# A two-layer hybrid encoder on one core: gate projections moved ahead of a norm, output projections moved into the sliding attention, and a decay matrix built by selection

## The chip, the cores and the metric

The kernel runs on one core of a Trainium2 chip. The metric is the device time of one execution in microseconds (us); the median of three runs counts. A core has TensorE (PE, matrix products), VectorE (DVE), ScalarE (ACT) and GpSimd (POOL), each with its own queue of instructions that it works off in order, and SyncE (SP), whose queue issues most of the DMA transfers.

## The reference

Two groups of tokens (1024 of a prompt, 512 of a sample, width 1024, fp32) go through two layers and a last RMSNorm. Cut to what matters here:

```python
# layer 0
u = rmsnorm(x) @ w_in                          # glu, a_gate, q, k, v, b_gate
a = a_val * sigmoid(a_glu)
a = layernorm(depthwise_conv(a, 31 taps))      # over channels
a = silu(a) * silu(a_gate)
o = windowed_gqa(rope(q), rope(k), v, sink) * silu(b_gate)   # +-128 tokens
x = x + concat([a, o]) @ w_out
# layer 1
u = rmsnorm(x) @ w_in                          # q, k, v, c_gate, z, xbc, dt_f, dt_b
c = diff_attention(q, k, v, lam) * silu(c_gate)
d = mamba2_bidir(z, xbc, softplus(dt_f + b), softplus(dt_b + b))
x = x + concat([c, d]) @ w_out
# in mamba2_bidir, per block of 128 tokens and direction (the backward one on flipped tokens)
decay[l, s] = exp(a_cum[l] - a_cum[s]) if l >= s else 0
y_diag = (C B^T * decay) @ (x * dt)            # and y = y_f + y_b + x * d_skip
```

## The kernel before

The 1536 tokens form three chunks of 512: g = 0 and 1 are the prompt, g = 2 the sample. Every fp32 product is split into high and low halves: the projection of one chunk onto 128 columns is 8 x 3 = 24 matmuls of 128 x 512 (`proj`, lines L294 to L296: high by high, high weight by low input, low weight by high input). `load_w` brings the weights in two halves (DMA), ACT rounds the high half (L282) and POOL subtracts the low half (L283). `split_into` does the same for inputs: ACT copies (L215), DVE or POOL subtracts (L216).

The program is written in phases, each with a set of SBUF and PSUM pools (`PHASES`, numbers of buffers per name). A tile scheduler decides the order on each engine from what is written; a buffer that is not yet free delays whoever wants it next.

Phase A1 computes the gated input, the convolution (taps on DVE and ACT, its last sum in L486), q, k and v, then the convolution's norm (`conv_ln`: first a matmul with a mean matrix, L494) and the first two groups of gates, `ag(0)` and `ag(1)`; a group is 128 channels for three chunks, 72 matmuls.

Phase A2 is the sliding attention: `swa_units` gives 24 units (12 blocks of 128 queries, two key heads), each of which computes scores (L568, L569), their row maximum (DVE, L572), exponentials (ACT, L574), scales them (POOL, L582), and for the unit before it transposes (L597), splits (L216) and multiplies with the values (L600, L601). The sample's 8 units come first, then the prompt's 16. `spread` puts other work between the units: groups of gates (`ag`, `bg`), and for `so[g]`, the output projection of chunk g, first the loading and multiplying of its 8 input tiles (`so[g][1]`, `cat_units`: two loads from DRAM, L626 and L629, a product on DVE, L630, and the split) and then its 8 projections (`so[g][2]`, 192 matmuls; L643 loads the residual, L644 adds, L654 squares, L655 sums the squares). The numbers in the table passed to `spread` are the units between which the work is written. The attention's output goes through DRAM (L605) before `cat_units` reads it.

Phase B1a does the rest of the output projections, each followed by `out_norm` (the next layer's norm: L668 loads, L669 scales, L216 splits), then `dtproj` (the 16 step sizes, on 40 columns, 24 matmuls per chunk) and the `xbc` projections. B1z holds two groups of token-major projections. B1b is the state-space scan, with projections of layer 1's attention between its blocks. Per block (12 of them) and direction, two matmuls (L872) write the exponents of 4 heads each into PSUM (`sg`), a second matmul with the identity adds a large negative number in the half that is to vanish (L873), ACT takes the exponential of all 8 heads (L876, 1024 columns), DVE adds the two directions (L878) and multiplies with C B^T (L883); 8 matmuls with x follow (L888). B2 is the differential attention and O1 the last output projection.

## Time and profile before

| | |
|---|---|
| median of three runs | 1650.86 us (1645.56, 1650.86, 1658.24) |
| the profiled execution | 1646.57 us |
| its span, first to last instruction | 1644.8 us |
| PE, DVE, ACT, POOL busy | 94%, 66%, 45%, 41% |
| mean granted clock of PE | 0.987 |

The profile is of one execution. Busy shares are means over stages of different kinds; the table of busy time by stretch parts them. An engine's idle time is given with the instruction that ended it. Matmuls overlap, so the time of one is longer than the step from one start to the next. The granted clock is a share of the full 2.4 GHz.

### The profile page before, as it was taken

Reading aid. Unit: us, or ns where it says so; the run is one execution under the profiler, and the core shown is the slowest. Engines: PE = TensorE matmul, PEld = TensorE weight load, DVE = VectorE, ACT = ScalarE, POOL = GpSimd, SP = SyncE. Lnnn points to the kernel's source line nnn. Section 1 sums busy time; section 2 is a strip of 40 time slices with the busy share of each in tenths; the row PEclk is TensorE's granted clock in tenths of the full one; section 3 lists DMA queues with packets and bytes.
Section 4 is the critical chain, followed back from the end, with each engine's and each line's share of the span. In section 5 each row is a group of like instructions: output and inputs, shape, how many; then the busy total and the mean of one; then the engine's idle time right before and its main releaser. Section 6 shows DMA issues by size and latency. Waiting matters only on the chain.

```text
span 1644.8 us, 22557 instructions
## 1 busy us (share of the span) xinstructions
PE 1541.7 (94%) x7772; PEld 1280.1 (78%) x7772; DVE 1092.4 (66%) x1568; ACT 747.4 (45%) x1461; POOL 670.8 (41%) x555
## 2 busy tenths in 40 slices
PE   4999899699989899999999999999989999999897
PEld 3888787478857777778788888878878888888787
DVE  6699999866688857565542005786537678678663
ACT  6312111266777754345442112222227777668532
POOL 4333543226766647432211006654435535341530
PEclk9999999899999999999999999999999999999999
DMA  9221123244556558613333217754454445342561
GB/s 371 70 68 42 45 84 92 94 159 143 162 172 192 167 165 264 203 58 91 112 126 116 77 45 218 212 173 152 133 172 139 142 152 167 116 133 73 182 232 67
DMA packets 159108, 229.43 MB, mean 139 GB/s; under 512 B 18279, under 2 KB 70567, under 8 KB 158994
## 3 DMA queue, kind: packets, MB, share of 16 engines
q1 hardware_dynamic: 157074, 227.40, 43.8%
q8 instruction: 61, 1.00, 0.3%
q0 software_dynamic: 1920, 0.59, 0.2%
q14 instruction: 53, 0.43, 0.1%
HBM read 153.15 MB, written 64.55 MB: 132 GB/s over the span
## 4 chain that ended last, share of the span: by engine, by line
PE 34%; DMA 5%; DVE 4%; issue 3%; ACT 2%; POOL 2%; SPq 1%; POOLq 0%; DVEq 0%; ACTq 0%
PE pj L294 4%; PE pj L295 4%; PE pj L296 4%; PE ms L994 3%; PE pjx L759 2%; PE pjx L760 2%; PE pjx L761 2%; PE s L978 2%; PE s L979 2%; PE pjx L296 2%; PE pjx L295 2%; PE pjx L294 2%; PE tr L406 1%; PE trx L406 1%; DMA ct<-g2d 1%
## 5 line engine op out<-in xcount | busy, mean ns | idle before, releaser
L283 POOL TENSOR_TENSOR wl<-wr,wh 128x512 fp32r<-128x512 f32 (+1 forms) x147 | 210.1, 1433 | 277.7 <-ACT wh L282 265.6
L295 PE MATMUL pjx<-x,wh 128*128 128x512 f32 (+1 forms) x576 | 227.6, 395 | 5.6 <-DVE x L216 5.6
L294 PE MATMUL pjx<-x,wh 128*128 128x512 f32 (+1 forms) x576 | 228.3, 397 | 3.0 <-DVE e L395 1.0
L296 PE MATMUL pjx<-x,wl 128*128 128x512 f32 (+1 forms) x576 | 227.7, 396 | 3.3 <-POOL wl L283 3.3
L294 PE MATMUL pj<-x,wh 128*128 128x512 f32 x536 | 215.8, 403 | 12.5 <-ACT e L387 4.4
L295 PE MATMUL pj<-x,wh 128*128 128x512 f32 x536 | 211.8, 395 | 4.5 <-DVE x L216 4.5
L296 PE MATMUL pj<-x,wl 128*128 128x512 f32 x536 | 213.1, 398 | 0.0
L282 ACT ACTIVATE wh<-wr 128x512 fp32r<-128x512 f32 (+1 forms) x147 | 91.5, 623 | 130.5 <-PE pjx L295 49.4
L295 PEld LDWEIGHTS pjx<-x,wh 128*128 128x128 f32 (+1 forms) x576 | 107.4, 186 | 30.8 <-DVE x L216 6.8
L294 PEld LDWEIGHTS pj<-x,wh 128*128 128x128 f32 x536 | 101.8, 190 | 37.1 <-ACT e L387 6.4
L294 PEld LDWEIGHTS pjx<-x,wh 128*128 128x128 f32 (+1 forms) x576 | 107.3, 186 | 29.3 <-ACT x L215 1.8
L296 PEld LDWEIGHTS pjx<-x,wl 128*128 128x128 f32 (+1 forms) x576 | 107.1, 186 | 28.0 <-POOL wl L283 4.1
L295 PEld LDWEIGHTS pj<-x,wh 128*128 128x128 f32 x536 | 101.7, 190 | 25.9 <-DVE x L216 6.0
L296 PEld LDWEIGHTS pj<-x,wl 128*128 128x128 f32 x536 | 101.7, 190 | 21.5 <-issue 0.5
L980 DVE TENSOR_REDUCE nmx<-s 128x1 f32<-128x1024 f32 (+1 forms) x96 | 97.9, 1040 | 23.5 <-PE s L979 23.0
L982 ACT ACTIVATE pr<-s,nmx 128x1024 f32<-128x1024 f32 (+1 forms) x96 | 93.4, 975 | 32.7 <-DVE nmx L980 29.1
L191 POOL TENSOR_TENSOR r<-v,mhalf 128x4 f32<-128x4 f32 (+2 forms) x37 | 33.4, 901 | 128.8 <-DVE v L187 76.5
L994 PEld LDWEIGHTS ms<-v,pT 128*128 128x128 f32 x640 | 78.5, 191 | 6.8 <-ACT m L996 2.0
L994 PE MATMUL ms<-v,pT 128*128 128x128 f32 x640 | 81.3, 276 | 2.2 <-ACT m L996 1.2
L532 POOL TENSOR_TENSOR raw<-raw,q 128x1024 fp32r<-128x1024 f32 x24 | 59.1, 2462 | 49.3 <-ACT q L530 38.7
L836 POOL TENSOR_TENSOR xd<-x,ed 128x512 f32<-128x512 f32 x20 | 23.2, 1161 | 125.5 <-DMA x<-xbd 120.6
L283 POOL TENSOR_TENSOR wlx<-wrx,whx 128x512 fp32r<-128x512 f32 x20 | 51.4, 2578 | 55.4 <-ACT whx L282 55.4
(415 smaller groups left out, 3786.9 us busy)
## 6 DMA issues: line engine op xcount, KB each, us to landing
wr<-in_wo SPq DMA_DIRECT2D x84, 256.0 KB, 4.2
wr<-in_w SPq DMA_DIRECT2D x71, 256.0 KB, 3.6
x<-xbd SPq DMA_DIRECT2D x22, 384.0 KB, 4.4
ct<-x1d SPq DMA_DIRECT2D x29, 256.0 KB, 4.3
raw<-q0d SPq DMA_DIRECT2D x48, 128.0 KB, 3.1
ct<-cat0d SPq DMA_DIRECT2D x24, 256.0 KB, 4.7
x1d<-e SPq DMA_DIRECT2D x24, 256.0 KB, 3.9
raw<-q1d SPq DMA_DIRECT2D x48, 128.0 KB, 2.8
```

Source lines behind the costliest of these rows:

```text
L191: G.tensor_tensor(out=r[:, 0:n], in0=v[:, 0:n], in1=mhalf[:, 0:n], op=ALU.pow)
L282: S.activation(out=wh, in_=raw, func=AF.Copy)
L283: G.tensor_tensor(out=wl, in0=raw, in1=wh.bitcast(F32), op=ALU.subtract)
L294: T_.matmul(acc, wh[:, kk, :], xh[:, k, :], start=(k == ks[0]), stop=False)
L295: T_.matmul(acc, wh[:, kk, :], xl[:, k, :], start=False, stop=False)
L296: T_.matmul(acc, wl[:, kk, :], xh[:, k, :], start=False, stop=(k == ks[-1]))
L406: T_.transpose(pt[:, t, :], src[:, t * P:(t + 1) * P], ident)
L532: G.tensor_tensor(out=lo, in0=raw, in1=q.bitcast(F32), op=ALU.subtract)
L759: T_.matmul(acc, xh[:, k, ts], hi[k], start=(k == 0), stop=False)
L980: V.tensor_reduce(out=nmx[:, t:t + 1], in_=o, axis=AX.XY, op=ALU.max, negate=True)
L982: S.activation(out=pr, in_=o, func=AF.Exp, bias=nmx[:, t:t + 1], accum_out=den[:, t:t + 1])
L994: T_.matmul(oacc, pT[:, i, :], vtok[:, kt, :], start=(kt == 0), stop=(kt == NB - 1))
```

## The change

1. The gate group `ag(2)` is written with `ag(0)` and `ag(1)` ahead of the convolution's norm, and the first mean matmul is tied to come after the last matmul of these three groups; `ag(3)` follows.
2. In A2 the pools change, the work between units is tied to the first score matmul of the unit written last, and its table changes: chunk 2's output projections come at 13 to 20, chunk 0's input tiles at 18 to 21 and its 8 projections at 20 to 26 (before: in B1a). Chunk 0's norm factor is computed at the end of A2.
3. `dtproj` packs the high and low weights into 128 columns, so that a chunk takes 16 matmuls; ACT copies the lower part of the result and DVE adds it.
4. In B1b the identity matmuls go. Both directions' exponents of 4 heads are written to two PSUM tiles, DVE copies the backward ones over the forward ones where a constant mask says so (`copy_predicated`, 128 x 512), and ACT takes one exponential of the result; the sum of the two directions goes. The diagonal of the backward direction is added to `d_skip`: two DVE reductions over C B^T times the identity and two small POOL operations per block. `rk` has four buffers for two.
5. Two constant tiles that served the identity matmuls are no longer made.

The core of the diff (left out: constants, the packing of the dt weights on the host, the copy of `rk` four times for two):

```diff
-    "A2": (dict(raw=3, v2=1, k4=3, v4=1, ct=3, ss=1, m2=1, sq=1, pT=5, pr=10, q6=2), dict(pjx=1, s1=3, trx=1)),
+    "A2": (dict(raw=3, q6=2, k2=2, v2=1, m2=1, pr=9, pT=5, k4=2, v4=1, ct=3, ss=2, sq=1), dict(pjx=1, s1=3, trx=1)),
...
-    "B1b": (dict(e2x=1, wrx=1, whx=1, wlx=1, rk=2, lk=4, cs=2, p4=4, x3=2, bc=2, xd=2, y=2, t=1, nx=4, pb=1, yc=2, zt=1), dict(sg=1, msx=2, trx=1)),
+    "B1b": (dict(e2x=1, wrx=1, whx=1, wlx=1, rk=4, lk=4, cs=2, p4=2, jk=1, x3=2, bc=2, xd=2, y=2, t=1, nx=4, pb=1, yc=2, zt=1), dict(sg=2, msx=2, trx=1)),
...
-                T_.matmul(acc, wl[:, kk, :], xh[:, k, :], start=False, stop=(k == ks[-1]))
+                ph["proj"] = T_.matmul(acc, wl[:, kk, :], xh[:, k, :], start=False, stop=(k == ks[-1]))
...
-    def conv_ln():
+    def conv_ln(pin):
         sm = cvs["s"]
         for g in GO:
             mu = pm("ms")
-            T_.matmul(mu, mean_w, sm[:, g, :], start=True, stop=True)
+            with tc.issue_after(pin.ins):
+                T_.matmul(mu, mean_w, sm[:, g, :], start=True, stop=True)
...
-            kt = sb("k4", (P, T), F32R)
+            kt = sb("k2" if T == CH and "k2" in ph["sb"] else "k4", (P, T), F32R)
...
-                T_.matmul(o, qh[:, g, j, :], kk[g][:, k0 * P:k1 * P], start=True, stop=False)
+                first = T_.matmul(o, qh[:, g, j, :], kk[g][:, k0 * P:k1 * P], start=True, stop=False)
                 T_.matmul(o, ql[:, g, j, :], kk[g][:, k0 * P:k1 * P], start=False, stop=True)
+                if j == 0:
+                    ph["pin"] = first
...
+    def norm_r(st_):
+        st_["r"] = rstd_of(tok_sum([st_["ss"]]), 4, 1.0 / DM)
+
     def out_norm(st_, spill, g, gcol, last):
-        bc = tok_bcast(rstd_of(tok_sum([st_["ss"]]), 4, 1.0 / DM), 4, False)
+        if "r" not in st_:
+            norm_r(st_)
+        bc = tok_bcast(st_["r"], 4, False)
...
-        wd = load_w(wdt, 40)
+        wd = {}
+        for i in range(2):
+            raw = sb("wr", (P, HK, P))
+            dma(out=raw, in_=wdt[:, HK * i:HK * i + HK, :])
+            w = sb("wh", (P, HK, P), F32R)
+            S.activation(out=w, in_=raw, func=AF.Copy)
+            G.tensor_tensor(out=w[:, :, 64:128], in0=raw[:, :, 64:128], in1=w[:, :, 64:128].bitcast(F32), op=ALU.subtract)
+            wd[i] = w
         xb, e, u = (sb("dt", (P, 3, CH))[0:40] for _ in range(3))
         for g in GO:
-            V.tensor_scalar(out=xb[:, g, :], in0=proj(wd, xn[g], 40), scalar1=prm[0:40, PC_DTB:PC_DTB + 1], scalar2=None,
-                            op0=ALU.add)
+            xh, xl = xn[g]
+            acc = pm("pj")
+            for k in range(KT):
+                w = wd[k // HK][:, k % HK, :]
+                lo = lambda: T_.matmul(acc[0:64], w[:, 0:64], xl[:, k, :], start=False, stop=False)
+                if k == KT - 1:
+                    lo()
+                T_.matmul(acc, w, xh[:, k, :], start=(k == 0), stop=(k == KT - 1))
+                if k < KT - 1:
+                    lo()
+            S.activation(out=u[:, g, :], in_=acc[64:104], func=AF.Copy)
+            V.scalar_tensor_tensor(out=xb[:, g, :], in0=acc[0:40], scalar=prm[0:40, PC_DTB:PC_DTB + 1], in1=u[:, g, :],
+                                   op0=ALU.add, op1=ALU.add)
...
-            es = []
+            rl = []
             for f in range(2):
                 c = cyc["n"] = (cyc["n"] + 1) % 4
-                sg = pm("sg", (P, 8, P))
-                r = rk[c % 2]
+                r, l = rk[c], lk[c]
                 G.dma_start(out=r[32:35], in_=acd[f, :, 8 * (b0 + b):8 * (b0 + b) + 8, :])
-                G.dma_start(out=lk[c][0:12], in_=nld[f, 2 * (b0 + b):2 * (b0 + b) + 2].rearrange("a r l -> r a l"))
-                for h in range(2):
-                    o = sg[:, 4 * h:4 * h + 4, :]
-                    T_.matmul(o, lk[c][:, h, :], r[:, 4 * h:4 * h + 4, :], start=True, stop=False)
-                    T_.matmul(o, ident_r, (neg_lo if f == 0 else neg_hi).unsqueeze(1).to_broadcast([P, 4, P]),
-                              start=False, stop=True)
-                e = sb("p4", (P, 8, P))
-                S.activation(out=e, in_=sg, func=AF.Exp)
-                es.append(e)
-            V.tensor_tensor(out=es[0], in0=es[0], in1=es[1], op=ALU.add)
+                G.dma_start(out=l[0:12], in_=nld[f, 2 * (b0 + b):2 * (b0 + b) + 2].rearrange("a r l -> r a l"))
+                rl.append((r, l))
+            e = sb("p4", (P, 8, P))
+            for h in range(2):
+                hs = slice(4 * h, 4 * h + 4)
+                sg = [pm("sg", QUAD) for _ in range(2)]
+                for o, (r, l) in zip(sg, rl):
+                    T_.matmul(o, l[:, h, :], r[:, hs, :], start=True, stop=True)
+                V.copy_predicated(out=sg[0], mask=m_gt.bitcast(I32).unsqueeze(1).to_broadcast([P, 4, P]), data=sg[1])
+                S.activation(out=e[:, hs, :], in_=sg[0], func=AF.Exp)
             cb = pm("tr", (P, 2, P))
             for g in range(2):
                 T_.matmul(cb[:, g, :], bc[:, g, :], bc[:, 2 + g, :], start=True, stop=True)
-            mv = es[0].rearrange("p (g h) l -> p g h l", g=2)
+            cbd, c8 = tiny(2, "cbd"), tiny(8, "c8")
+            for g in range(2):
+                V.tensor_tensor_reduce(out=sb("jk", (P, P)), in0=cb[:, g, :], in1=ident, scale=1.0, scalar=0.0, op0=ALU.mult,
+                                       op1=ALU.add, accum_out=cbd[:, g:g + 1])
+            G.tensor_tensor(out=c8.rearrange("p (g h) -> p g h", g=2),
+                            in0=d_t[:, 1, b0 + b, :].rearrange("p (g h) -> p g h", g=2),
+                            in1=cbd.unsqueeze(2).to_broadcast([P, 2, 4]), op=ALU.mult)
+            G.tensor_tensor(out=c8, in0=c8, in1=rows[:, RW_DS:RW_DS + 8], op=ALU.add)
+            mv = e.rearrange("p (g h) l -> p g h l", g=2)
             V.tensor_tensor(out=mv, in0=mv, in1=cb.unsqueeze(2).to_broadcast([P, 2, 4, P]), op=ALU.mult)
             y = sb("y", HEADS)
-            G.tensor_tensor(out=y, in0=x8, in1=bch(rows[:, RW_DS:RW_DS + 8]), op=ALU.mult)
+            G.tensor_tensor(out=y, in0=x8, in1=bch(c8), op=ALU.mult)
             yd = pm("ms", HEADS)
             for h in range(8):
-                T_.matmul(yd[:, h, :], es[0][:, h, :], x8[:, h, :], start=True, stop=True)
+                T_.matmul(yd[:, h, :], e[:, h, :], x8[:, h, :], start=True, stop=True)
...
-    def spread(a, groups):
+    def spread(a, groups, pin=False):
         at = [[] for _ in range(len(a) + 1)]
         for f, p0, p1 in groups:
             for i, u in enumerate(f):
                 at[min(len(a), p0 + i * (p1 - p0) // len(f))].append(u)
         for i, u in enumerate(a):
-            run(at[i])
+            run(at[i], pin)
             u()
-        run(at[-1])
+        run(at[-1], pin)
...
-    def run(us):
+    def run(us, pin=False):
         for u in us:
-            u()
+            with tc.issue_after(ph["pin"].ins) if pin and "pin" in ph else nullcontext():
+                u()
...
-    conv_ln()
-    run(ag(0) + ag(1))
+    run(ag(0) + ag(1) + ag(2))
+    conv_ln(ph["proj"])
+    run(ag(3))
 
     phase("A2")
     res0 = lambda g, j: xin(g)[:, j, :]
     so = [out_units(wo0, lambda st_, g=g: cat_units(st_, catd[0], {k: gd[k // 4] for k in range(8)}, g), res0, x1d, g, 4) for g in range(3)]
     uS, uP = swa_units(1), swa_units(0)
     spread(uS + uP, [
-        (ag(2) + ag(3) + bg(0) + bg(1) + bg(2, (2,)) + bg(3, (2,)), 0, 7),
-        (so[2][1], 11, 19),
-        (bg(2, (0, 1)) + bg(3, (0, 1)), 9, 17),
-        (so[0][1], 19, 19),
-        (so[2][2], 21, 26)])
+        (bg(2, (2,)) + bg(3, (2,)) + bg(0) + bg(1), 0, 9),
+        (so[2][1], 9, 14),
+        (bg(2, (0, 1)) + bg(3, (0, 1)), 9, 13),
+        (so[2][2], 13, 20),
+        (so[0][1], 18, 21),
+        (so[0][2], 20, 26)], True)
     out_norm(so[2][0], x1d, 2, PC_G1, False)
+    norm_r(so[0][0])
 
     phase("B1a")
-    run(so[0][2])
     run(so[1][1])
```

The order of instructions shows the change at three places. The first is PE at the end of phase A1. In the rows of the kernel before, `pj_2480` is the result of the first projection of `ag(2)`, `msx_2056` that of the norm's first mean matmul:

```order
L296 MATMUL pj_2480<-x_37_246,wl_2439 128x512
L294 MATMUL pj_2480<-x_37_246,wh_2438 128x512
L295 MATMUL pj_2480<-x_38_247,wh_2438 128x512
L494 MATMUL msx_2056<-y_153_1256,mean_w 128x512
L296 MATMUL pj_2480<-x_37_246,wl_2439 128x512
```

In the changed kernel `pj_2337` is the result of the last projection of `ag(2)`, and `pjx_2498` belongs to what comes next:

```order
L295 MATMUL pj_2337<-x_47_294,wh_2270 128x512
L296 MATMUL pj_2337<-x_48_295,wh_2270 128x512
L297 MATMUL pj_2337<-x_47_294,wl_2271 128x512
L491 MATMUL msx_2368<-y_153_1253,mean_w 128x512
L295 MATMUL pjx_2498<-x_31_209,whx_2487 128x512
```

The mean matmul stood between the fifth and the sixth matmul of `ag(2)`; now it stands behind all 72.

The second is PE at the end of the sliding attention. Before, `ms_5302` collects the last unit's value products, and `pjx_5526` and `pjx_5570` are chunk 0's output projections:

```order
L295 MATMUL pjx_5526<-x_800_4377,wh_5519 128x512
L600 MATMUL ms_5302<-pT_5308,v_578_3581 128x512
L601 MATMUL ms_5302<-pT_5309,v_578_3581 128x512
L600 MATMUL ms_5302<-pT_5319,v_578_3581 128x512
L296 MATMUL pjx_5526<-x_799_4376,wl_5520 128x512
L294 MATMUL pjx_5570<-x_799_4376,wh_5557 128x512
L601 MATMUL ms_5302<-pT_5320,v_578_3581 128x512
L295 MATMUL pjx_5570<-x_800_4377,wh_5557 128x512
```

In the changed kernel the last projection of chunk 0 is `pjx_5562`, `s_1102` and `s_1104` are the last two score tiles of the last unit:

```order
L600 MATMUL ms_5511<-pT_5529,v_584_3597 128x512
L599 MATMUL ms_5511<-pT_5539,v_584_3597 128x512
L297 MATMUL pjx_5562<-x_841_4611,wl_5556 128x512
L565 MATMUL s_1102_5606<-k_582_3592,q_1034_5357 128x256
L566 MATMUL s_1102_5606<-k_582_3592,raw_5352 128x256
L600 MATMUL ms_5511<-pT_5540,v_584_3597 128x512
L565 MATMUL s_1104_5612<-k_582_3592,q_1034_5357 128x256
L566 MATMUL s_1104_5612<-k_582_3592,raw_5352 128x256
L596 MATMUL tr_5629<-cst,pr_5481 128x128
```

and the attention ends so, with `ms_5653` as the last value product, `ms_5679` and `ms_5688` of a norm factor and `pjx_5905` as chunk 1's first projection:

```order
L596 MATMUL trx_5665<-cst,pr_5615 128x128
L599 MATMUL ms_5653<-pT_5659,v_584_3597 128x512
L600 MATMUL ms_5653<-pT_5660,v_584_3597 128x512
L599 MATMUL ms_5653<-pT_5670,v_584_3597 128x512
L600 MATMUL ms_5653<-pT_5671,v_584_3597 128x512
L199 MATMUL ms_5679<-ones,ss_3961 128x1 x4
L206 MATMUL ms_5688<-cst,r_5686 128x128 x4
L295 MATMUL pjx_5905<-x_1139_5786,wh_5892 128x512
```

Chunk 0's projections stood around and behind the last value products; now all of them stand ahead of the last two score tiles, and nothing but two small sums stands between the last value product and chunk 1's projections.

The third is DVE in the state-space scan. Before, at one block, `p_1542` is the matrix of the 8 heads, `tr_8530` the product C B^T, `nx` are states:

```order
L847 TENSOR_TENSOR nx_8351<-nx_8351,msx_8348 128x512
L846 TENSOR_TENSOR nx_8422<-nx_8351,ed 128x512
L878 TENSOR_TENSOR p_1542_8518<-p_1542_8518,p_1544_8527 128x1024
L883 TENSOR_TENSOR p_1542_8518<-p_1542_8518,tr_8530 128x1024
L847 TENSOR_TENSOR nx_8411<-nx_8411,msx_8408 128x512
L395 SCALAR_TENSOR_TENSOR e_1563_8606<-pj_8579,cs_8292 128x512
```

In the changed kernel, at the same block, `sg_8509` and `sg_8510` are the exponents of the two directions for heads 4 to 7, and `p_1541` is the matrix:

```order
L868 TENSOR_TENSOR nx_8409<-nx_8338,ed 128x512
L898 COPY_PREDICATED sg_8509<-cst,sg_8510 128x512
L912 TENSOR_TENSOR p_1541_8502<-p_1541_8502,tr_8515 128x1024
L869 TENSOR_TENSOR nx_8398<-nx_8398,ms_8395 128x512
L391 SCALAR_TENSOR_TENSOR e_1568_8599<-pj_8572,cs_8273 128x512
L898 COPY_PREDICATED sg_8618<-cst,sg_8619 128x512
L869 TENSOR_TENSOR nx_8409<-nx_8409,msx_8406 128x512
```

The sum of the directions of 1024 columns is gone, and a masked copy of 512 columns stands there, with a second one further ahead for heads 0 to 3.

## Rows read from the trace of the kernel before

**Rows 1.** The page, part 1: busy us (share of the span) and instructions of each engine.
```profile
PE 1541.7 (94%) x7772; PEld 1280.1 (78%) x7772; DVE 1092.4 (66%) x1568; ACT 747.4 (45%) x1461; POOL 670.8 (41%) x555
```

**Rows 2.** Busy time by stretch; columns in the first line.
```profile
core 0: us, PE busy (x) PEld busy (x) DVE busy (x) ACT busy (x) POOL busy (x), PEclk, DMA share, GB/s
...
305.50:319.30 13.80, 0.82 (x4) 0.36 (x2) 13.73 (x15) 2.80 (x5) 1.58 (x1) 0.67 0.15 57
319.30:378.10 58.80, 57.66 (x261) 46.35 (x262) 34.71 (x48) 31.74 (x51) 17.95 (x12) 0.96 0.52 173
378.10:609.00 230.90, 213.00 (x1063) 172.07 (x1062) 168.92 (x386) 163.31 (x396) 148.23 (x173) 0.99 0.54 162
609.00:689.80 80.80, 76.94 (x346) 62.96 (x345) 53.20 (x75) 35.81 (x63) 50.51 (x37) 0.98 0.76 238
...
992.00:1238.60 246.60, 235.04 (x1169) 196.34 (x1168) 153.43 (x206) 68.04 (x108) 124.60 (x133) 1.00 0.58 174
```

**Rows 3.** Timeline of PE, 303 to 328 us: start us, us, instruction, [idle before, releaser].
```profile
305.93 0.39 PE L295 MATMUL pj<-x,wh 128*128 128x512 f32 x1
319.39 2.07 PE L494 MATMUL msx<-y,mean_w 128*128 128x512 f32 x2 [13.07 <-DVE y L486]
320.48 1.42 PE L296 MATMUL pj<-x,wl 128*128 128x512 f32 x1
...
326.59 0.39 PE L294 MATMUL pjx<-x,wh 128*128 128x512 f32 x1
```

**Rows 4.** Busy time by stretch, within the attention; columns as in rows 2.
```profile
463.00:502.00 39.00, 30.45 (x139) 21.32 (x138) 33.10 (x80) 29.05 (x76) 23.33 (x32) 0.96 0.51 152
...
557.00:579.00 22.00, 16.72 (x81) 12.07 (x80) 20.11 (x53) 17.70 (x45) 12.24 (x17) 0.92 0.47 146
```

**Rows 5.** Timeline of DVE, 604 to 650 us; columns as in rows 3.
```profile
617.63 0.69 DVE L630 SCALAR_TENSOR_TENSOR ct<-ct,ct 128x512 f32<-128x512 f32 x1 [2.34 <-DMA ct<-g1d]
...
638.75 2.80 DVE L216 TENSOR_TENSOR x<-ct,x 128x512 fp32r<-128x512 f32 x2
```

**Rows 6.** Timeline of PE, 642 to 646 us.
```profile
644.38 0.39 PE L294 MATMUL pjx<-x,wh 128*128 128x512 f32 x1
```

**Rows 7.** Timeline of PE, 686 to 692 us.
```profile
685.70 0.39 PE L294 MATMUL pjx<-x,wh 128*128 128x512 f32 x1
...
689.55 0.40 PE L296 MATMUL pjx<-x,wl 128*128 128x512 f32 x1
689.78 0.40 PE L294 MATMUL pjx<-x,wh 128*40 128x512 f32 x1
...
691.88 0.40 PE L294 MATMUL pjx<-x,wh 128*40 128x512 f32 x1
```

**Rows 8.** Groups by line, 992 to 1238.6 us: count, busy us, mean ns, idle before.
```profile
L873 PE MATMUL sg<-cr 128*128 128x512 f32 x48 | 19.2, 400 | 0.0
...
L878 DVE TENSOR_TENSOR p<-p,p 128x1024 f32<-128x1024 f32 x12 | 16.0, 1332 | 7.3 <-ACT p L876 7.3
...
L883 DVE TENSOR_TENSOR p<-p,tr 128x1024 f32<-128x1024 f32 x12 | 14.6, 1217 | 0.4
...
L889 DVE TENSOR_TENSOR y<-y,msx 128x512 f32<-128x512 f32 x9 | 6.1, 683 | 6.4 <-PE msx L888 6.0 <-POOL y L885 0.3
```

**Rows 9.** Line L216, all of the span: duration ns min/median/max, first and last start.
```profile
L216 DVE TENSOR_TENSOR x<-ct,x x38: 661/689/1790, 418.5 to 1553.2; 128x512 fp32r<-128x512 f32 x38
L216 DVE TENSOR_TENSOR pT<-tr,pT x32: 659/686/694, 396.1 to 601.3; 128x512 fp32r<-128x512 f32 x32
```

**Rows 10.** Groups by line and shape, 378.1 to 609 us; columns as in rows 8.
```profile
L283 POOL TENSOR_TENSOR wl<-wr,wh 128x512 fp32r<-128x512 f32 x33 | 45.6, 1391 | 18.1 <-ACT wh L282 13.4 <-PE tr L597 1.9 <-ACT es L578 1.4
...
L630 DVE SCALAR_TENSOR_TENSOR ct<-ct,ct 128x512 f32<-128x512 f32 x19 | 15.8, 831 | 11.3 <-DMA ct<-g0d 6.7 <-DMA ct<-g1d 4.5
...
L388 DVE SCALAR_TENSOR_TENSOR e<-e,e 128x512 f32<-128x512 f32 x11 | 13.9, 1263 | 4.8 <-ACT e L387 4.7
...
L655 DVE TENSOR_TENSOR ss<-ss,sq 128x512 f32<-128x512 f32 x8 | 9.7, 1210 | 1.4 <-ACT sq L654 1.2
```

20 lines of the change are left out of this document (8 added, 12 removed).

## The prediction

> **What bounds it now.** I read the page first: TensorE (PE) is busy 94% of the span [rows 1], so time can come only from matmuls that vanish and from stretches in which PE stands still. The busy times by stretch tell where those are. From PE's first score matmul of the sliding attention (378.1 us) to its last attention matmul (609.0) PE is busy 213.0 of 230.9 us; from there to the first dt matmul (689.8) 76.9 of 80.8; in the state-space phase (992.0 to 1238.6) 235.0 of 246.6 [rows 2]. Next I read PE's own timeline around the convolution's norm: a matmul starts at 305.93, the next, the norm's first mean, at 319.39, and the 13.07 us between are put down to VectorE's (DVE's) last convolution instruction, L486 [rows 3]. PE's granted clock is 0.67 in that hole [rows 2], and the 18 matmuls from 320.48 to 326.59 then take 6.1 us [rows 3]. At full rate matmuls of 512 columns start 0.2265 us apart (17 steps from 685.70 to 689.55, [rows 7]), so 18 would take 4.1.
>
> A second kind of idle lies within the attention: 8.6 us in 463 to 502 and 5.3 us in 557 to 579, where DVE is busy 33.1 of 39.0 and 20.1 of 22.0 [rows 4]; the latter holds three attention units without projections beside them, 7.3 us each. A third item is hidden today: the last attention output goes to DRAM and comes back as input of chunk 1's projections. The first product of what comes back runs at 617.63, 8.6 us after the last attention matmul, and the last splits end at 641.55 [rows 5]; chunk 1's first projection matmul starts at 644.38 [rows 6]. PE does chunk 0's projections meanwhile.
>
> **The change in the order on PE.** I count projection matmuls (of 512 columns) per stretch in the order of both programs:
> start to first mean: 1157, now 1224 (+67); mean to first score: 206, now 120 (-86); first score to last attention matmul: 486, now 624 (+138); from there to the first dt matmul: 311, now 192 (-119). The sum of the four is unchanged. So the rearrangement only shifts work, and its gain is the idle time that it covers less the idle that it opens.
>
> *Start to mean.* 67 matmuls are 15.2 us, and they run in the place of the hole; the matmul at 305.93 is the fifth of the group's 72, so the mean would start at 305.93 + 68 x 0.2265 = 321.3, two microseconds after DVE's last convolution instruction released it before. PE's step from 305.93 to 319.39 is 13.46 us for one step of 0.23, so 13.2 us of idle goes: +15.2 - 13.2 = +2.0. The gates of the eighth and ninth projection queue on DVE behind the convolution's last instructions; that delays the norm's subtractions by about 1.6 us and no matmul. I leave it out.
>
> *Mean to first score.* 86 matmuls less are -19.5 us. The slow clock after the hole goes with it, 6.1 - 4.1 = 2.0 us, and of the idle in this stretch (58.8 - 57.7 = 1.1) I take 1.0: **-22.5**.
>
> *First score to last attention matmul.* 138 more matmuls are +31.3 us. Against that, projections are spread better: before, units 9 to 12 and 20 to 22 have none between their scores, seven units of 23; now there are three without. The 8.6 us hole at 463 to 502 stands where chunk 2's projections wait step by step for their splits; they now start some units after their loads, and I take 6 of it. In the last unit, chunk 0's matmuls stand ahead of the last two scores, so the softmax, transposes and value matmuls behind them have no cover; the bare pace is 7.3 us, some 4 of it without PE work; units 20 to 22 get 40 projection matmuls and give about that back. Net idle -6: **+25.3**. Bounds: -14 (both holes go) to +12 (holes stay, and the tail and a second bare unit come on top).
>
> *To the first dt matmul.* What is left is chunk 1's 192 matmuls, 43.5 us, and about 2 us of transposed sums. Nothing covers the trip to DRAM any more. Its bounds: 8.6 us to the first product, 0.69 for it and as much for the copy behind it, 10 us, if the splits keep pace with PE; or, with DVE's queue as it is, the last split at 641.55, 32.6 us after the last attention matmul, with 7 projections still to do (38.1): 72.7 in all. DVE has less between them than before, because the squares of chunk 0 are done earlier and part of chunk 2's norm, too; I take 14 us of idle, near the lower end. 43.5 + 2 + 14 = 59.5 against 80.8: **-21.3** (from -25 to -8). The four sum to 2.0 - 22.5 + 25.3 - 21.3 = -16.5.
>
> **dt projections.** 72 matmuls become 48, spaced 0.233 us today (689.78 to 691.88, nine steps, [rows 7]): 24 x 0.233 = **-5.6**. The added copy on ScalarE and the sum on DVE per chunk lie beside the projections that PE goes on with (uncovered they would be two operations of about 0.7 us for the last chunk). A longer preparation of the weights, twice 512 columns on ScalarE and on GpSimd (POOL), must end before 670; it is loaded early. I take -5.5, range -6 to -4.
>
> **State-space decay.** 48 identity matmuls go (L873, 48 in [rows 8]): 48 x 0.2265 = 10.9 us of PE. DVE loses the sum of the two directions (L878, 16.0 us). It gains 24 masked copies of 512 columns in PSUM, for which no row exists. Bounds: 0.68 us, the row of the same size that reads PSUM (L889), and 1.22, the 1024 columns of L883; being 512 columns I take the former, with a bound to 1.22: 16.4 to 29.3 us. 24 reductions of 128 columns cost at most 0.68 each and by their size half: 8 us. DVE goes from 153.4 [rows 2] to about 162, at most 183, of 236 us, so it isn't the bound over the stretch. But scores, masked copy, exponential, product and matmul now pass DVE's in-order queue twice per half instead of once; behind a waiting masked copy stand gates and state updates for which PE waits. I give 1.5 us back: **-9.5**, range -13 to 0.
>
> **Sum.** -16.5 - 5.5 - 9.5 = -31.5. The profiled execution took 1646.57, so 1615.1; the median of the runs shown is 4.3 above it, and I take half of that: **1617**.
>
> **Rivals.**
> *The hole only moves* (0.19). For it: in the attention DVE, ScalarE and POOL are at 64 to 73% together with PE at 92% [rows 2], and the trip to DRAM now lies bare. Against: three empty units instead of seven. If the idle it opens equals the 16.5 us that it saved, only the 15.0 us of removed matmuls stay: 1634.
> *The masked copies bind* (0.10): at 1.22 us, or with DVE's queue in the way, the state-space phase keeps its 246.6 us: 1617 + 9.5 = 1626.
> *It goes better* (0.08): 10 us at the junction and both holes filled, 1617 - 4 - 8 = 1605 or below.
> *Slower, by the shared port* (0.08). In this kernel a DVE operation on two tensors in SBUF is sometimes stretched: the split of ct, 689 ns in the middle, goes up to 1790, while the same instruction that reads PSUM never leaves 659 to 694 [rows 9]. Beside it, POOL works on weights and splits. Products of two loaded tiles (831 ns mean), sums of squares (1210) and gates (1263) show the same [rows 10]. The stretch from 378.1 to 689.8 has 80 such operations in the changed kernel (25 splits, 24 products, 21 sums of squares, 10 gates; 78 before), 1.00 us on average by the rows; the 138 more matmuls are nearly six projections, whose twelve weight subtractions on POOL (1391 ns each, [rows 10]) now lie among the attention, 16.7 us. If each of the 80 went to 1.79, DVE would have 63 us more. It decides from 31.5 us, that is when 40 of the 80 are stretched and on the path: then the time is that of before, 1648; with all of them 1680. Against it: DVE has room of 62 us in the attention [rows 2].
>
> The Trainium skill, "SBUF — State Buffer", section "SBUF: two separate sides", says that a DVE operation with two SBUF inputs and a POOL operation exclude each other for a whole instruction. By that rule this rival is a mechanism and not noise; the trace agrees in that only the form with two SBUF inputs is stretched (1790 against 694 ns).
>
> **Chances.** Forecast 0.55 (its own range 1607 to 1628). Faster by over 1%, about what a measurement of this kernel can tell from no change, means below 1634: the forecast, the better case, the masked copies, and half of the moved hole: 0.55 + 0.08 + 0.10 + 0.09 = 0.82; slower is half of the port rival, 0.04; the rest, 0.14, is within 1%. The range takes in the better case and the moved hole: 1600 to 1638.
>
> **What would show it.** Right: the first mean starts near 321 with no step over 1 us on PE before it and a clock of 1.00 after it; the first score near 357; the last attention matmul near 613; a hole of 10 to 16 us behind it, put down to the cat loads or their splits; dt near 673; the state-space phase 236 to 239 us long with masked copies near 0.7 us. Wrong: PE waits in units 8 to 22 that grow over 20 us, a hole over 20 us at the junction, masked copies over 1 us, or POOL and DVE rows that are longer than before in the same forms.

## The result and the profile after

The changed kernel takes 1661.07 us (median of 18 runs) against 1649.85 of the kernel before: ratio 1.0074, 95% interval 1.0061 to 1.0087. It is slower by three quarters of a per cent; forecast were 1617 us and a range from 1600 to 1638. The profiled execution took 1661.53 us.

The page of the changed kernel, its span, PE's line and the granted clock in 40 slices:

```profile
span 1659.7 us, 22440 instructions
...
PE 1556.5 (94%) x7700; PEld 1284.8 (77%) x7700; DVE 1090.9 (66%) x1630; ACT 744.2 (45%) x1466; POOL 676.0 (41%) x579
...
PEclk9999999999899997999999999999999999999999
```

PE runs 72 instructions less and is busy 14.8 us longer than in [rows 1]. That alone says that a part of the loss is neither a wait nor a moved instruction: matmuls take longer. The busy times by stretch (columns as in [rows 2], cut at the same places of the program: first mean, first score, last attention matmul, first dt matmul, first state matmul of the scan, first score of the differential attention):

```profile
0.00:322.10 322.10, 295.22 (x1261) 238.31 (x1262) 290.91 (x325) 90.45 (x149) 124.43 (x68) 0.99 0.32 107
322.10:356.80 34.70, 34.70 (x167) 28.13 (x166) 23.70 (x41) 24.47 (x41) 13.88 (x10) 1.00 0.45 144
356.80:629.60 272.80, 251.48 (x1208) 202.25 (x1207) 186.15 (x401) 181.94 (x421) 162.63 (x184) 0.97 0.57 177
629.60:693.80 64.20, 56.12 (x227) 44.34 (x225) 42.10 (x65) 27.64 (x47) 33.70 (x26) 0.82 0.67 217
693.80:993.20 299.40, 297.31 (x1356) 241.16 (x1355) 105.56 (x131) 101.83 (x142) 54.36 (x34) 1.00 0.30 94
993.20:1241.20 248.00, 228.94 (x1098) 188.95 (x1096) 160.94 (x269) 57.66 (x107) 132.91 (x157) 0.97 0.56 171
1241.20:1659.70 418.50, 392.74 (x2392) 341.68 (x2392) 281.53 (x401) 260.23 (x561) 154.11 (x103) 0.99 0.43 137
```

Against the prediction's terms (elapsed us; the last column is the changed kernel with 64 bytes of padding, `after_pad` below):

| stretch | before | forecast | measured | after_pad |
|---|---|---|---|---|
| start to first mean | 319.4 | 321.3 | 322.1 | 321.8 |
| to first score | 58.7 | 36.2 | 34.7 | 34.4 |
| to last attention matmul | 230.9 | 256.2 | 272.8 | 269.8 |
| to first dt matmul | 80.8 | 59.5 | 64.2 | 63.0 |
| to first state matmul | 302.2 | 296.7 | 299.4 | 296.9 |
| scan | 246.6 | 237.1 | 248.0 | 246.8 |
| rest | 406.2 | 406.2 | 418.5 | 416.1 |
| sum (span) | 1644.8 | 1613.2 | 1659.7 | 1648.8 |

One stretch of one profile is good to a few us: the kernel before and `before_pad` (below), which run the same order, differ by 3.6 us up to the first mean (319.4 and 323.0). The first two terms came out. The 46 us between forecast and measurement (1613.2 and 1659.7) are in the attention (+16.6), behind it (+4.7), in dt (+2.7), in the scan (+10.9) and in the rest (+12.3). The first mean stands where the order put it, without a step over 1 us ahead of it (timeline of PE):

```profile
321.82 0.39 PE L297 MATMUL pj<-x,wl 128*128 128x512 f32 x1
322.05 1.02 PE L491 MATMUL msx<-y,mean_w 128*128 128x512 f32 x2
322.51 0.79 PE L295 MATMUL pjx<-x,whx 128*128 128x512 f32 x1
```

### The profile page after: what moved, and what is told of

The parts are those of the page before. It is cut to its first block, busy times and chain, and to the rows that moved or that the text cites. A ratio compares the mean times of both kernels' runs of the same rounds, so it can differ in the third digit from the quotient of the medians.

```text
span 1659.7 us, 22440 instructions
## 1 busy us (share of the span) xinstructions
PE 1556.5 (94%) x7700; PEld 1284.8 (77%) x7700; DVE 1090.9 (66%) x1630; ACT 744.2 (45%) x1466; POOL 676.0 (41%) x579
## 5 line engine op out<-in xcount | busy, mean ns | idle before, releaser
L284 POOL TENSOR_TENSOR wl<-wr,wh 128x512 fp32r<-128x512 f32 x143 | 207.0, 1450 | 248.1 <-ACT wh L283 230.9
L295 PE MATMUL pj<-x,wh 128*128 128x512 f32 x532 | 217.6, 409 | 14.4 <-ACT e L383 7.5
L296 PE MATMUL pjx<-x,wh 128*128 128x512 f32 x532 | 214.2, 403 | 5.7 <-DVE x L217 5.1
L296 PE MATMUL pj<-x,wh 128*128 128x512 f32 x532 | 214.5, 403 | 4.4 <-DVE x L217 4.3
L295 PE MATMUL pjx<-x,wh 128*128 128x512 f32 x532 | 214.4, 404 | 3.7 <-ACT x L216 3.7
L297 PE MATMUL pjx<-x,wl 128*128 128x512 f32 x532 | 213.5, 402 | 0.0
L283 ACT ACTIVATE wh<-wr 128x512 fp32r<-128x512 f32 x143 | 89.3, 628 | 117.6 <-PE pjx L296 52.8
L296 PEld LDWEIGHTS pjx<-x,wh 128*128 128x128 f32 x532 | 101.7, 191 | 30.6 <-DVE x L217 6.7
L295 PEld LDWEIGHTS pjx<-x,wh 128*128 128x128 f32 x532 | 102.1, 192 | 26.4 <-ACT x L216 4.0
L297 PEld LDWEIGHTS pjx<-x,wl 128*128 128x128 f32 x532 | 101.5, 191 | 22.9
L733 DVE SCALAR_TENSOR_TENSOR y<-a,prm,y 128x1536 f32<-128x1536 f32 x32 | 60.9, 1904 | 29.4 <-ACT y L730 28.9
```

What stands on the lines that cost most here:

```text
L283: S.activation(out=wh, in_=raw, func=AF.Copy)
L284: G.tensor_tensor(out=wl, in0=raw, in1=wh.bitcast(F32), op=ALU.subtract)
L295: T_.matmul(acc, wh[:, kk, :], xh[:, k, :], start=(k == ks[0]), stop=False)
L296: T_.matmul(acc, wh[:, kk, :], xl[:, k, :], start=False, stop=False)
L297: ph["proj"] = T_.matmul(acc, wl[:, kk, :], xh[:, k, :], start=False, stop=(k == ks[-1]))
L733: V.scalar_tensor_tensor(out=acc, in0=a[:, :, t:t + CH], scalar=prm[:, wc + t:wc + t + 1], in1=acc, op0=ALU.mult, op1=ALU.add)
```

## Experiments

### The parts alone

Four kernels take the kernel before and put single parts of the change into it. Theory A: every part's gain or loss is its own. Theory B: the parts act on each other. The first piece is that of `p1_gates`, and of `p13_gates_dt`, which has part 3 as well; the line behind it stands in the table of `p2_attention`, which otherwise has part 2 as it is; `p4_decay` has part 4 as in the diff of the change.

```diff
-    conv_ln()
-    run(ag(0) + ag(1))
+    run(ag(0) + ag(1) + ag(2))
+    conv_ln(ph["proj"])
+    run(ag(3))
...
-        (ag(2) + ag(3) + bg(0) + bg(1) + bg(2, (2,)) + bg(3, (2,)), 0, 7),
+        (bg(0) + bg(1) + bg(2, (2,)) + bg(3, (2,)), 0, 7),
```

```diff
+        (ag(2) + ag(3) + bg(2, (2,)) + bg(3, (2,)) + bg(0) + bg(1), 0, 9),
```

> The kernel before with part 1 alone: ag(2) and ag(3) are written around the convolution's norm, the first mean matmul is tied behind the last gate matmul, and the attention's own table and pools stay (without ag(2) and ag(3) in it). Theory A, each part's loss or gain is local: the 13 us hole goes and nothing is given back, 1636 to 1640 us. Rival B, the parts act on each other: the gates missing from the attention bare its units, which takes 8 to 13 us back there, 1645 to 1650.

> The kernel before with part 2 alone: the attention's table, its pools, the tied work between units and the early norm factor, with ag(2) and ag(3) still written into the attention. Theory A: the changed kernel reaches dt 5.6 us later than before although it saved 13 us ahead of the attention, so part 2 alone costs about 18 us, 1664 to 1670. Rival B: with the 144 gate matmuls as further cover the part costs less than 8 us, 1650 to 1658.

> The kernel before with part 4 alone: masked copy for identity matmuls in the state-space scan. Theory A: the loss after 992 us is the part's own; the stretch from the first state matmul to the end is 13.7 us longer in the changed kernel, so 1660 to 1666, with drops of the granted clock in the scan. Rival B: the loss there comes from what the other parts shift, and the part alone gives what its 48 matmuls weigh, 1638 to 1643.

> The kernel before with parts 1 and 3: the gate group ahead of the norm, and the packed dt projections. Theory A: 13 + 5 us, 1631 to 1636. Rival B: part 3's 5 us alone, 1643 to 1647.

Measured, with the kernel before at 1646.76: `p1_gates` 1637.98 (ratio 0.9955, 0.9938 to 0.9971), `p2_attention` 1656.91 (1.0068, 1.0053 to 1.0084), `p4_decay` 1650.70 (1.0028, 1.0008 to 1.0047), `p13_gates_dt` 1633.98 (0.9937, 0.9916 to 0.9958). Part 1 keeps nearly all of its gain, part 3 adds 4 us to it (the difference of two kernels; it was not run alone), part 2 loses 10 us and not 18, part 4 loses 4 although 48 matmuls are gone. The four sum to about +1; together they made +11 to +14. So A held for parts 1 and 3, part 2 lies in the range of B, though it lost more than the 8 us that B allowed, and part 4 lies between the two. Something acts between the parts.

### One part taken out, and two edits of the attention

`p123` is the change without part 4, `p134` the change without part 2. `after_nopin` is the changed kernel without the ties:

```diff
-        (so[0][2], 20, 26)], True)
+        (so[0][2], 20, 26)])
```

`after_cover` keeps half of chunk 0's eight output projections for the time behind the attention:

```diff
-        (so[0][2], 20, 26)], True)
+        (so[0][2][:4], 20, 26)], True)
-    norm_r(so[0][0])
...
     phase("B1a")
+    run(so[0][2][4:])
```

> The changed kernel without part 4 (the decay is built as before, by identity matmuls). Theory A, the parts add: alone they gave -9, +10, +4 and about -4, so this one comes to about 1645 to 1650. Theory C, the masked selection loses only beside part 2 (together the four measured +14, not the +1 of their sum): 1644 to 1648 too, with the stretch from the first state matmul to the end at 653 us as before (666.5 in the changed kernel). Against both: 1655 or more, if that stretch is long without part 4 as well.

> The changed kernel without part 2 (attention table, pools and ties as before). Theory A, the parts add: 1634 + 4, 1636 to 1641, with the stretch from the first state matmul to the end near 650 as in part 4 alone. Theory D, the order in the state-space scan is drawn anew with whatever precedes it, and its time moves by several us either way without a cause in the parts: that stretch anywhere from 648 to 666, so 1634 to 1652.

> The changed kernel with its table and pools, but the work between the attention units is not tied to their score matmuls. If the ties hold the loads of the prompt's keys and values back in SyncE's queue behind gate stores (ScalarE waits 6.0 and 3.0 us for them at 405 to 413, and PE stands for 11.5 us between 400 and 425), the hole goes and the time falls by 6 to 12 us, 1649 to 1655. If the pools are the cause, the hole stays, and the time is within 3 us of 1661.

> The changed kernel with the last four of chunk 0's eight output projections written behind the attention again (96 matmuls, 21.7 us), and its norm factor with them. If the bare end of the attention and the trip to DRAM cost for want of cover (PE lost 24 us between 615 and 650, with the granted clock at 0.56), 14 to 20 us come back: 1641 to 1647. If DVE and GpSimd are what that stretch waits for, the matmuls only move and it gives less than 5.

Measured, beside 1646.11 of before: `p123` 1645.55 (0.9989, 0.9974 to 1.0003), `p134` 1644.08 (0.9982, 0.9966 to 0.9999), `after_nopin` 1659.04 (1.0077, 1.0053 to 1.0101), `after_cover` 1644.90 (1.0004, 0.9982 to 1.0027).

By the ratios, adding part 4 costs 14 us on `p123`, 7 us on `p13_gates_dt` and 5 on the kernel before: it never pays as it stands, with the addresses that it brings (below). `p123` fits both of its theories. `p134` misses the sum of the parts (1636 to 1641). In `p123` scan and rest take 656.9 us, in `p134` 655.8, in the changed kernel 666.5.

The ties are the cause of one hole, and not of the loss. In the changed kernel's attention PE is idle longest in 400 to 425 us (6.9 us); without the ties the hole goes and others open: the attention takes 268.1 us for 272.8, and the two medians can't be told apart (busy time by stretch, first the changed kernel, then `after_nopin`):

```profile
400.00:425.00 25.00, 18.14 (x81) 14.46 (x80) 15.80 (x31) 16.65 (x38) 15.48 (x15) 0.84 0.53 141
```

```profile
400.00:425.00 25.00, 23.92 (x116) 18.74 (x115) 15.62 (x33) 16.01 (x38) 16.72 (x16) 1.00 0.42 127
...
450.00:475.00 25.00, 20.73 (x100) 15.58 (x99) 19.58 (x50) 19.49 (x53) 14.75 (x21) 0.93 0.63 192
...
600.00:625.00 25.00, 21.22 (x102) 16.52 (x101) 14.64 (x36) 13.66 (x35) 9.78 (x15) 0.86 0.63 204
```

How the first hole comes about is read from the waits of the changed kernel (engine, what waited, releaser: us in total, times, longest):

```profile
SPq L385 <- DVE den L579: 8.8, 1, 8.8
```

```profile
ACT k L516 <- DMA raw<-k0d: 6.0, 1, 6.0
ACT v L543 <- DMA raw<-v0d: 3.0, 1, 3.0
```

```profile
PE ms L599 <- DVE m L602: 5.8, 2, 3.7
```

and from DVE's timeline:

```profile
396.41 2.07 DVE L384 SCALAR_TENSOR_TENSOR e<-e,e 128x512 f32<-128x512 f32 x1 [4.29 <-ACT e L383]
...
398.59 0.18 DVE L579 RECIPROCAL den<-den 128x4 f32<-128x4 f32 x1
```

A store of a gate (L385) stands at the head of SyncE's queue for 8.8 us by the row, until DVE ends the gate's last step (L384) at 398.5 us; the row names the reciprocal behind it, but the store is issued at 398.51, before that ends. Two loads of keys (`k0d`) stand behind it and are issued from 399.0 on. So ScalarE stands at the keys (6.0) and, as the loads of the values follow at 408.4, at the values (3.0), with the attention's output behind them in its queue, and PE waits for that. In the kernel before such a store stands there 5.9 us at most, and ScalarE waits less for keys and never for values (waits from 378.1 to 609 us; L389 is the store, L519 the keys):

```profile
SPq L389 <- DVE e L388: 21.4, 8, 5.9
```

```profile
ACT k L519 <- DMA raw<-k0d: 2.2, 1, 2.2
```

Without the ties ScalarE still waits 4.5 us for keys and 2.6 for values, but PE has other matmuls then and does not stand. I had looked at PE, DVE and ScalarE for what each filler displaces, and not at SyncE.

`after_cover` brings 16 us by the medians and 12 by the ratios, about what was expected for want of cover; but the trace gives only part of it there. First score to first dt matmul falls from 337.0 to 328.2 us, while scan and rest, whose code is the same, fall from 666.5 to 654.0; the scheduler gives them another order in the two kernels. The total came out, and not by the mechanism alone.

### The operands' addresses

The clue is in the time of one matmul. The changed kernel ahead of its first dt matmul, where nothing waits (timeline of PE), and then the same place with the padding described below:

```profile
685.63 0.39 PE L296 MATMUL pjx<-x,wh 128*128 128x512 f32 x1
...
693.57 0.39 PE L297 MATMUL pjx<-x,wl 128*128 128x512 f32 x1
```

```profile
680.85 0.39 PE L295 MATMUL pjx<-x,wh 128*128 128x512 f32 x1
...
688.78 0.39 PE L297 MATMUL pjx<-x,wl 128*128 128x512 f32 x1
```

34 steps in 7.94 us, 233.5 ns, against 35 in 7.93, 226.6, which is the step of [rows 7]. All kernels with part 4 and without the padding have the longer step, already in the first 100 us, where no instruction of part 4 has run. What part 4 changes there is where things lie: its two new small tiles (`cbd`, `c8`) take 192 bytes in each partition ahead of the pool `x16` of the projections' inputs. In the compiled program of before, `x16` begins at 46656 and the weights `wh` at 22848, 23808 = 93 x 256 apart; in the changed one at 45312 and 21312, 24000 = 93 x 256 + 192. The kernel has a constant of 8 floats, `pad`, that is never read; making it longer moves `x16` and all behind it, and leaves the order of the instructions the same.

`before_pad`, `after_pad`, `cover_pad` and `p134_pad` have 24 floats there, on the kernel before, the changed one, `after_cover` and `p134`; `p13_128` has 40, on `p13_gates_dt`:

```diff
-    V.memset(tiny(8, "pad", 1), 0.0)
+    V.memset(tiny(24, "pad", 1), 0.0)
```

> The kernel before with its constant named pad 64 bytes longer (24 floats for 8); the order of all instructions is that of before, only the addresses of the inputs of the projections and of all later buffers move by 64 bytes in each partition. Theory E, the step between two matmuls depends on whether their stationary and moving operands agree modulo 128 bytes (in the kernels without part 4 they agree and the step is 227 ns; in those with part 4 two thirds of the pairs differ by 64 and their step is 233): 2900 matmuls x 5.5 ns, about 16 us slower, 1660 to 1666, steps of 233 ns with the first weight pool. Rival F, the longer step comes from part 4's instructions: no change, within 2 us of the kernel before.

> The changed kernel with the same 64 bytes, which bring its operands back into agreement; same order. Theory E: steps of 227 ns everywhere and 13 to 18 us less, 1643 to 1648. Rival F: 1659 to 1663.

> The changed kernel with half of chunk 0's projections behind the attention and with the 64 bytes. If the two causes are separate, their gains add: 1645 - 15, 1627 to 1632. If the aligned steps only bare more waits, less than 8 us: 1637 or more.

> The changed kernel without part 2, with the 64 bytes: gate group, packed dt and masked selection over the old attention. Theory E: 1644 - 15, 1626 to 1631, below parts 1 and 3 without masked selection (1634), so that part 4's own gain shows. If part 4 has no gain of its own, 1633 or more.

> Parts 1 and 3 (1634.0) with 128 bytes more ahead of the inputs of the projections, so that input and weight addresses of the first weight pool differ by 128 bytes modulo 256 (0 before, 64 in before_pad with steps of 229.3 ns, 192 in the changed kernel with 233.2). The same order. If the step grows with the distance, it is 231 ns or so and the time 1637 to 1642. If 128 bytes are as good as 0, 1632 to 1636 and 227 ns. If another distance than 0 is better still, less than 1630 and steps under 225 ns.

Measured, beside 1645.66 (1645.88 for the last): `before_pad` 1647.44 (1.0002, 0.9985 to 1.0019), `after_pad` 1651.85 (1.0031, 1.0015 to 1.0047), `cover_pad` 1640.90 (0.9976, 0.9958 to 0.9993), `p134_pad` 1635.58 (0.9954, 0.9911 to 0.9997), `p13_128` 1640.79 (0.9981, 0.9963 to 0.9998).

With the padding the changed kernel gains 7 us by the ratios (9 by the medians), `p134` and `after_cover` 5 each (8.5 and 4), the last two with intervals that overlap: less than the 13 to 18 that I expected. PE's busy time falls from 1556.5 to 1540.0 us in the changed kernel and the span by 10.9, so the other 5.6 us became waits. The opposite edit costs: `p13_128` has 128 bytes more than `p13_gates_dt` and is 7 us slower, as expected for a step that grows with the distance. Theory E in its form, agreement modulo 128 bytes, fell with `before_pad`, which differs by 64 and loses nothing that can be told; rival F fell with `p13_128`, which has the longer step and no part 4. What holds in all of them is the distance from a matmul's input to the weights modulo 256 bytes (means over steps between matmuls of 512 columns, of steps under 245 ns, matched with the addresses of the compiled program):

| distance mod 256 | kernel | steps | mean ns |
|---|---|---|---|
| 0 | p1_gates | 4516 | 227.9 |
| 0 | after_pad | 4602 | 228.0 |
| 64 | before_pad | 2964 | 229.3 |
| 128 | p13_128 | 2914 | 232.5 |
| 192 | the changed kernel | 2939 | 233.2 |
| 0 | the changed kernel, weights in the pools `whx` and `wlx` | 649 | 227.5 |

Two groups of weights in one execution, 227.5 and 233.2, and the same weights with and without the padding, in one order, 228 and 233.2, leave the distance as the difference: neither the address of the inputs alone nor that of the weights alone parts these rows. 2939 x 5.2 ns are 15 us of PE work, of which 7 to 9 came back. Why the distance matters is not shown.

### Why the missing matmuls of the scan bring so little

With the addresses mended, `p134_pad` still only equals `p13_gates_dt`. Two more kernels from it. `decay_fill` does every exponent matmul twice:

```diff
                 for o, (r, l) in zip(sg, rl):
-                    T_.matmul(o, l[:, h, :], r[:, hs, :], start=True, stop=True)
+                    for _ in range(2):
+                        T_.matmul(o, l[:, h, :], r[:, hs, :], start=True, stop=True)
```

`decay_nomask` has no masked copy; it leaves out the backward half of the matrix:

```diff
-                V.copy_predicated(out=sg[0], mask=m_gt.bitcast(I32).unsqueeze(1).to_broadcast([P, 4, P]), data=sg[1])
-                S.activation(out=e[:, hs, :], in_=sg[0], func=AF.Exp)
+                S.activation(out=e[:, hs, :], in_=sg[0], func=AF.Exp, scale=0.001)
```

> p134_pad (gate group, packed dt, masked selection, operands in agreement) with each of the 48 exponent matmuls issued twice in a row, to the same values: 48 x 0.2265 = 10.9 us of PE work come back into the state-space scan. Theory G, the identity matmuls had lain in time that PE waits there anyway: within 3 us of p134_pad (1635.6), 1633 to 1639, with PE's idle in the scan some 10 us less. Rival H, PE's work bounds the scan: 1644 to 1648.

> p134_pad without the masked copy: both directions' exponents are still computed, but the exponential reads the forward ones alone (with a scale of 0.001, so that it stays finite), so the backward half is left out. DVE loses 24 instructions of 0.69 us, and the chain from the exponents to the matrix one engine. Rival H (what was gained on PE is lost because the chain now waits for DVE): 6 to 10 us faster than p134_pad, 1626 to 1630. Theory G (the scan is bound by the rest of its chain): within 3 us, 1633 to 1638.

Measured, beside 1645.88: `decay_fill` 1639.54 (0.9960, 0.9940 to 0.9979), `decay_nomask` 1638.69 (0.9962, 0.9941 to 0.9984). Busy times of the scan and of the rest in `p13_gates_dt`, `p134_pad`, `decay_fill` and `decay_nomask`, in this order:

```profile
977.40:1224.50 247.10, 237.71 (x1169) 198.66 (x1168) 152.96 (x206) 68.27 (x109) 127.11 (x134) 0.99 0.56 174
1224.50:1631.80 407.30, 385.50 (x2369) 338.75 (x2367) 280.80 (x400) 260.62 (x559) 155.45 (x102) 0.98 0.43 140
```

```profile
983.40:1220.80 237.40, 223.31 (x1097) 186.51 (x1095) 157.77 (x269) 57.16 (x107) 131.56 (x156) 0.98 0.58 179
1220.80:1633.80 413.00, 390.34 (x2392) 340.84 (x2392) 283.19 (x401) 260.05 (x561) 153.12 (x103) 0.99 0.43 139
```

```profile
982.60:1228.00 245.40, 233.22 (x1146) 195.06 (x1144) 159.84 (x269) 57.20 (x107) 131.14 (x156) 0.98 0.57 173
1228.00:1637.50 409.50, 389.48 (x2392) 341.04 (x2392) 282.03 (x401) 260.19 (x561) 154.16 (x103) 0.99 0.44 140
```

```profile
984.20:1230.80 246.60, 230.57 (x1098) 192.44 (x1096) 141.81 (x245) 55.47 (x105) 131.90 (x157) 0.94 0.57 173
1230.80:1641.00 410.20, 389.30 (x2393) 340.35 (x2392) 284.69 (x401) 262.15 (x562) 155.99 (x103) 0.99 0.44 140
```

The masked selection shortens the scan by 9.7 us, close to the 9.5 of the prediction, and the rest grows by 5.7. That is 24 projections (5.4 us): the order has 624 projection matmuls in the scan of before and 600 in every kernel with part 4, so that 24 run in the differential attention. (It is 600 in `p2_attention` and `p123` as well, which have part 2 and not part 4: part 4 is not the only thing that moves them.) Over both, part 4 gains 4.0 us in the profile here (654.4 to 650.4) for 9.6 us less of busy PE, with 5 us more of idle in the scan. The total doesn't show it: `p134_pad` reaches the first state matmul 6.0 us later than `p13_gates_dt` (983.4 and 977.4), where PE runs the same matmuls in the same order in both. 48 matmuls put back (`decay_fill`) cost 4 us by the medians and 1 by the ratios, less than the interval of `p134_pad`, which was run five times. In the profile they are 9.9 us more of busy PE in the scan, which grows by 8.0 us, and the rest is 3.5 shorter. So in the scan itself only 1.9 us of that work lies in time that PE would wait, and theory G, which wanted some 10, is not shown; nor did the time rise to H's 1644. H's other form, that the chain waits for DVE, fell: without the masked copy DVE has 16 us less work, and the time is not shorter.

`decay_nomask` shows how far the time moves without work: less work on DVE, as many matmuls on PE, and a scan 9.2 us longer, 7.3 of them busy time, at a granted clock of 0.94 for 0.98. Why its clock is lower is not shown. In nine kernels with the code of part 4 scan and rest take between 649.8 us (`p4_decay`) and 666.5 (the changed kernel), in seven without it between 651.4 and 656.9. Of the nine, the six that have part 2 as well take 654.0 to 666.5, the three without it 649.8 to 655.8. `after_pad`, whose addresses are mended, has 662.9 there and `p134_pad` 650.4, and 10.4 us of that difference are idle time of PE (47.1 and 36.7 us); the two kernels run the scan's instructions in different orders. What makes the one order worse than the other I could not settle with an experiment.

### Cover for the trip to DRAM

```diff
 tail_cover, on after_pad
+                ph["val"] = T_.matmul(oacc, vtok[:, k0 + kb, g, :], pl_, start=False, stop=(kb == nk - 1))
...
-        (so[0][2], 20, 26)], True)
+        (so[0][2][:5], 20, 26)], True)
...
-    norm_r(so[0][0])
     phase("B1a")
+    with tc.issue_after(ph["val"].ins):
+        run(so[0][2][5:])
```

> The changed kernel with the 64 bytes (after_pad, 1651.9) and with the last three of chunk 0's projections tied behind the attention's last value matmul: 72 matmuls, 16.3 us, over the trip to DRAM. In after_pad PE loses 15.7 us there (8.6 us of gaps, 7.1 us of low clock). If want of cover is the cause, most of it comes back: 10 to 13 us less, 1638 to 1642. If DVE's queue of norm and splits is the cause, the matmuls only move: 1649 or more.

Measured 1642.25 us (0.9984, 0.9969 to 1.0000), 8 us less than `after_pad` by the two ratios, a little under the 10 to 13 expected. The stretch from the last attention matmul to the first dt matmul, in `after_pad` and in `tail_cover`:

```profile
626.00:689.00 63.00, 54.36 (x226) 43.98 (x226) 41.86 (x65) 27.59 (x47) 34.05 (x26) 0.84 0.67 224
```

```profile
614.70:685.20 70.50, 67.17 (x298) 53.72 (x297) 49.90 (x69) 31.95 (x56) 43.93 (x32) 0.98 0.73 238
```

72 matmuls more, 16.3 us, cost 7.5: gaps fall from 8.6 to 3.3 us and the clock is back at 0.98. So the hole there was want of cover. With this edit and the padding the changed kernel's loss against the kernel before is gone; against the 1617 us of the forecast 25 us are still missing.

## Why the prediction was wrong, point by point

Three steps failed: the attention's "Net idle -6" (idle grew by 3.4 us), the decay's "-9.5" (the scan grew by 1.4 us) with the rest taken as unchanged (12.3 us longer), and a term that the sum does not have, the step between matmuls, which the new buffers made longer (15 us of PE work, 7 to 9 us of the time).

**Start to mean, mean to first score.** Right in mechanism and size: 13.2 us of idle went, the clock behind it is 1.00, and `p1_gates` alone takes 9 us off the kernel.

**First score to last attention matmul.** The count of 138 matmuls was right; the step "Net idle -6" failed. Elapsed less busy went up from 17.9 to 21.3 us, so 9.4 of the 16.6 us missed are idle. The other 7.2 are busy time: it rose by 38.5 us, of which 138 matmuls at 0.2265 explain 31.3; the granted clock fell from 0.99 to 0.97, and the padding takes 3.0 us off the stretch. I had counted units without projections (seven before, three now) as a measure of idle. What stopped PE was a store at the head of SyncE's queue and the loads behind it, a queue that I named in no step, and the attention's end without cover. The first of these is only a part: with that hole gone (`after_nopin`) others opened, and what opens them is not shown.

**To the first dt matmul.** The hole was forecast, its size was not quite: 14 us of idle were taken. In the timeline of PE

```profile
629.61 0.63 PE L600 MATMUL ms<-pT,v 128*128 128x512 f32 x1
631.64 1.87 PE L199 MATMUL ms<-ones,ss 128*128 128x1 f32 x8 [1.40 <-DVE m L602]
634.87 2.08 PE L206 MATMUL ms<-cst,r 128*128 128x128 f32 x8 [1.36 <-POOL r L192]
640.64 1.22 PE L295 MATMUL pjx<-x,wh 128*128 128x512 f32 x2 [3.69 <-ACT x L216]
642.49 0.79 PE L296 MATMUL pjx<-x,wh 128*128 128x512 f32 x1 [0.64 <-POOL x L217]
```

chunk 1's first projection starts 11.0 us after the last attention matmul, within the 10 us of the lower bound and the 14 taken; the term that was missed is the clock, 0.82 over the stretch: the matmuls behind the hole run at half speed for some 10 us.

**dt projections.** -5.5 forecast, -5.3 in `after_pad`; -2.8 in the changed kernel, where the longer step takes the difference. Over the old attention it is less: from `p1_gates` to `p13_gates_dt` busy time falls by 5.4 us in this stretch and the elapsed time by 1.9, since PE then waits 3.4 us for the splits of its inputs.

**State-space decay.** The prices were right. The masked copy and the reduction (line, engine, operation, count: ns min/median/max):

```profile
L898 DVE COPY_PREDICATED sg<-cst,sg x24: 679/689/697, 1004.3 to 1199.7; 128x512 f32<-128x512 int32 x24
```

```profile
L905 DVE CUSTOM_DVE_ANT_0 jk<-tr,cst x24: 276/282/293, 999.0 to 1194.7; 128x128 f32<-128x128 f32 x24
```

DVE's busy time in the scan is 160.9 us, 162 was forecast. What failed is the step from "48 matmuls go" to "-9.5 on the path". Against the kernel before, 72 matmuls (16.3 us) are gone from the scan, but its busy time fell by 6.1 us only, since the clock (0.97 for 1.00) and the step are worse, and its idle rose by 7.5 (11.6 to 19.1). Two things were left out of the sum: 24 projections that left the scan for the next phase, which I had taken as unchanged at 406.2 us although the order shows them, and the idle that the rearranged order bared. PE's waits in the changed kernel's scan:

```profile
PE pj L295 <- DVE e L391: 5.2, 2, 2.7
PE pj L295 <- ACT e L383: 5.1, 1, 5.1
...
PE sg L897 <- DVE sg L898: 2.0, 1, 2.0
```

**What I did not think of.** The addresses: 7 to 9 us by `after_pad`, 10.9 of the 46 in the two profiles. The order of instructions says nothing of them, but the line that makes a constant that is never read stands in the kernel, and the two new small tiles stand in the diff.

**The rivals.** The masked copies don't bind (0.69 us). The hole did move, and more idle opened than this rival's 1634 us allowed for. The shared port is not the cause: the split of ct has 675/692/1781 ns now, as in [rows 9], and in the attention the products and sums of squares of [rows 10] take 871 and 995 ns, the gates 1256; from the first score to the first dt matmul the four forms together cost DVE 79 us, 82 before. That a rearranged stretch gets new idle of more than it saved, in three places at once, was no case of mine at all beyond 1634 us, where I had the port alone; the bounds of the terms (+12 for -6 in the attention, 0 for -9.5 in the scan) would have given 1617 + 18 + 9.5 = 1644.5, and the junction's (-8 for -21.3) 1658.

**The better version.** Parts 1 and 3 over the old attention and the old decay: 1633.98 us, by the ratios 0.6% below the kernel before and 1.4% below the changed one.

## What to carry to other kernels

A matmul that vanishes may bring less than its step, as here, where 9.6 us less of PE work in scan and rest made them 4.0 us shorter in the profiles; before it is booked as gain, count the idle of the stretch and ask what will wait in its place, SyncE's queue included. Where a change adds or resizes a buffer, however small, compare the addresses of weights and inputs before and after: 192 bytes changed the step of some 2900 matmuls here. Work that covers a trip to DRAM should stay tied behind the last instruction ahead of that trip, as in `tail_cover`.
